# The low part of each weight piece from ScalarE and an accumulating DMA instead of a VectorE subtraction

## The chip, the cores and the metric

The kernel runs on one core of a Trainium2 chip. The metric is the device time of one execution in microseconds (us), lower is better. The engines are named as in the profile: PE (TensorE matmul), PEld (TensorE weight load), DVE (VectorE), ACT (ScalarE), POOL (GpSimd), SP (SyncE).

## What is computed

Two transformer layers over 512 tokens of 1024 channels, float32, batch 1. In short, out of the reference:

```python
x = x + 0.5 * swiglu_ffn(rmsnorm(x, ffn1_norm), ffn1_w_gate, ffn1_w_up, ffn1_w_down)
x = x + hybrid_mixer(rmsnorm(x, mix_norm), w_in, ...)      # sparse attention and gated linear attention
x = x + 0.5 * swiglu_ffn(rmsnorm(x, ffn2_norm), ffn2_w_gate, ffn2_w_up, ffn2_w_down)
x = rmsnorm(x, final_norm)
# second layer: pooling branch and bidirectional mLSTM branch, gated, merged, projected, added to x
swiglu_ffn(x, g, u, d) = (silu(x @ g) * (x @ u)) @ d        # d_ff = 2816
```

Nearly all of the work is the product of activations with weight matrices.

## The kernel before

Channels lie on the partitions and the 512 tokens along the free dimension. TensorE multiplies in float32r, a rounded format. To keep float32 accuracy every operand is cut into a high part (`hi`, the value rounded to float32r) and a low part (`lo`, the rest), and `mm3` makes three matmuls of each product: hi by hi, weight-hi by activation-lo, weight-lo by activation-hi.

All weight matrices are cut on the host into pieces of 128x1024 in the order of use. `load` brings the next piece into a `raw` buffer through SP's DMA queue. `chunk` makes `whi` from it with a copy on ACT (line 107) and `wlo` with a subtraction on DVE (line 108). There are three buffers each of `raw`, `whi` and `wlo`. 253 pieces go through `chunk`; a few others are split elsewhere.

`Tiles.next` hands out the eight 128x128 weight tiles of a piece, one after the other, to `gemm_t`, which makes one 128-channel output of 512 tokens (lines 124 to 126 in `mm3`). So a piece lasts for 24 matmuls of 512 columns. `gemm_nat` takes two pieces at once, and walks over both of them twice, for two token tiles each time: 96 matmuls of 256 columns a pair of pieces. It is called nine times: for `gv` (twice), `gr` (twice), `vn` and `V` (twice two).

The framework's scheduler puts the instructions of each engine in an order of its own. Each engine then runs its instructions strictly in that order, and waits on semaphores for what it needs. The buffers set when a piece can be split: ACT may write the `whi` of a piece when the matmuls of the piece three before it are done, and SP may load into a `raw` buffer when the last reader of it is done.

The products' results go from PSUM through DVE and ACT: in the feed-forward part `ft` (gate times the norm's factor, then Silu), `fv` (up, times that) and `hdh`, `hdl` (the two parts of the product).

Of the kernel before, what the change touches and what calls it, by code (L numbers as in the profile page):

```python
# [10 lines left out]
F32 = mybir.dt.float32  # L11
F32R = mybir.dt.float32r
I32 = mybir.dt.int32
AF = mybir.ActivationFunctionType
ALU = mybir.AluOpType
AX = mybir.AxisListType

P = 128
# [9 lines left out]
MM_BANKS = 4  # L28
UP = 4  # the first up product starts this many tiles behind the gate product
FILL = (0, 2, 4, 6, 8, 10, 13, 16)  # the steps between the heads that carry other products  # L30

# columns of the packed per-channel vectors
VEC = {}
# [10 lines left out]
def kernel(  # L44
# [9 lines left out]
    nc = tc.nc  # L54
# [19 lines left out]

# [1 line left out]
    vs = cp.tile([P, NVEC], F32, name="vs")  # L76
# [16 lines left out]

# [1 line left out]
    state = {"n": 0}  # L95

    def load():
        raw = wp.tile([P, 1024], F32, tag="raw", name="raw", bufs=3)
        nc.sync.dma_start(raw, wst[state["n"]])
        state["n"] += 1  # L100
        return raw

    def chunk(raw=None):
        raw = raw or load()
        hi = wp.tile([P, 1024], F32R, tag="whi", name="whi")
        lo = wp.tile([P, 1024], F32R, tag="wlo", name="wlo")
        act.copy(hi, raw)  # L107
        dve.tensor_sub(lo, raw, hi.bitcast(F32))  # L108
        return hi, lo
# [18 lines left out]
    def gemm_t(tl, ah, al, name="g"):  # L128
        """psum[channel, token] of one 128-wide tile of output channels"""
        o = bank(name, "mm")  # L130
        n = len(ah)
        for k in range(n):
            wh, wl = tl.next()
            mm3(o, wh, wl, ah[k], al[k], k == 0, k == n - 1)
        return o

    def gemm_nat(ah, al, evac):
        """psum[token, channel] of 256 output channels, one token tile after the other"""
        c = [chunk(), chunk()]
        for i0 in range(0, NT, 2):  # L140
            outs = [bank(f"gn{i0 + i}", "mm") for i in range(2)]
            for k in range(KT):
                hi, lo = c[k // 4]
                cs = slice((k % 4) * 256, (k % 4 + 1) * 256)
                for i in range(2):
                    s = slice((i0 + i) * P, (i0 + i + 1) * P)
                    mm3(outs[i][:, :256], ah[k][:, s], al[k][:, s], hi[:, cs], lo[:, cs],
                        k == 0, k == KT - 1)
            for i in range(2):
                evac(i0 + i, outs[i][:, :256])  # L150

    def split(src, g, name, alloc):
        """hi/lo float32r parts of src * g (g a per-partition column or None)"""
        h, l = alloc(name + "h", F32R), alloc(name + "l", F32R)
        split_into(h, l, src, g)
        return h, l
# [8 lines left out]

# [1 line left out]
    def sq_acc(acc, src, first):  # L167
# [13 lines left out]
    def rsqrt_small(src, scale, name, shape=None):  # L181
        """1 / sqrt(src * scale + eps): shifted-exponent seed, three Newton steps"""
        sh = shape or [P, NT]
# [20 lines left out]

# [1 line left out]
    def new_acc():  # L206
# [30 lines left out]
    def normed(gname, acc):  # L237
        """evacuation that splits x * g for the next product and sums the squares"""
        ah, al = [], []

        def evac(d):
            a, b = split(x[d], vcol(gname, d), "x", xs)
            ah.append(a)
            al.append(b)
            sq_acc(acc, x[d], d == 0)
        return ah, al, evac

    # the first gate and up products run along with the loads of x and its split
    raws = []
# [20 lines left out]

    # a column of zeros that is there after the split: the squares come behind it
    zero = cp.tile([P, 1], F32, name="zero")
# [15 lines left out]

# [1 line left out]
    with ExitStack() as mx:  # L290
# [11 lines left out]

        # tables that depend on positions alone
        valid = mt("valid", shape=[P, 1])
# [15 lines left out]

# [1 line left out]
        hid = {}  # L322
# [3 lines left out]
        def compress_blocks(n):  # L326
            pe_n = pe_k if n == "k" else pe_v
            blk = [wtmp("blk", [P, 8, 2, 31]) for _ in range(2)]
            for g in range(2):
# [3 lines left out]
                nc.gpsimd.dma_start(st[64:128, 0:T - 1], src[:, 1:T])  # L333
                # blk[a][:, j, g, n] = st[:, 16 n + 2 (8 a + j)] + pe[:, 8 a + j]
                for a in range(2):
# [34 lines left out]
        with tc.tile_pool(name="gp", bufs=1) as gp:  # L370
# [10 lines left out]

            # 64 channels: both parts of their weights fit one tile, and two passes do
            gat = ga("gat", shape=[64, T])
# [14 lines left out]
            dve.tensor_mul(gat, t, rbc[:64])  # L398
            # decay: cumulative log_sigmoid within 64-token chunks (b) and 128-token pairs (bp)
            zs, es = [], []  # L400
            for c in range(2):
# [6 lines left out]
                zs.append(z), es.append(e)  # L408
            # gates, natural, sigmoid as 1 / (1 + exp(-z))
            o = bank("gt")  # L410
# [17 lines left out]
            for c in range(2):  # L428
# [4 lines left out]
                bp3 = bp.rearrange("p (n s) -> p n s", n=4)  # L433
                # q exp(b), k exp(b_last - b) of even chunks, k exp(bp_last - bp), k exp(-b), q exp(bp)
                qi, kn = ga(f"qin{c}"), ga(f"ktn{c}")
# [23 lines left out]

# [1 line left out]
            S = gt("S", [P, 2, P])  # L461
# [54 lines left out]

# [1 line left out]
            blk = {}  # L518
            for n in ("k", "v"):
                o = gemm_t(tl, ah, al)  # L520
                dve.tensor_mul(kcv[n], o, rbc)
                blk[n] = compress_blocks(n)
            # per head (hi; lo) of the query over 128 rows, (hi; hi) and (lo; lo) of the key
            # (a query carries 1 / slope of its head, so that one distance table serves all)
            def qk_tile(j):
# [39 lines left out]

            # gated, normalised, transposed
            for i in range(NT):
# [11 lines left out]
        with tc.tile_pool(name="np", bufs=1) as np_:  # L579
            # distances in units of 1 / slope: key - query (the query at the last tile), and of the blocks  # L580
            dist = np_.tile([P, T], F32, name="dist")
# [15 lines left out]

            # x += (gated linear attention's half of the output projection), between the heads
            def gla_out(d):
                o = gemm_t(tl, [ogl[0][:, c] for c in range(4)], [ogl[1][:, c] for c in range(4)], "wo")  # L600
                dve.tensor_add(x[d], o, x[d])

            # query tiles by bank: 3; 2 and 0; 1
            GRP = ((3,), (2, 0), (1,))
            OFF = {3: 0, 2: 512, 0: 896, 1: 1024}

            def probs(b, h):
                """exp of the shifted scores of one head, queries on the partitions"""
                j, e = h % 4, h // 4
# [45 lines left out]

# [1 line left out]
            def compressed(i):  # L657
# [40 lines left out]

            # heads 2 c and 2 c + 1 for the output projection
            no = {}  # L700
# [31 lines left out]

# [1 line left out]
            acc = new_acc()  # L734
# [22 lines left out]

# [1 line left out]
    mb = ctx.enter_context(tc.tile_pool(name="mb", bufs=1))  # L759
# [18 lines left out]

    # gates: rows 0-3 forward, 32-35 backward
    R = 36  # L780
# [28 lines left out]
    for src, dst in ((G, Gn), (F, En)):  # L809
        o = bank("gT")  # L810
# [3 lines left out]

    # values of two heads, natural, in two parts, with a column of ones per head
    def values2():
# [12 lines left out]

    # queries and keys: width-5 convolution along the tokens, silu  # L830
    def conv(c):
# [67 lines left out]

    # branch gate sigmoid(o) * silu(z_b)  # L900
    gate = []
# [31 lines left out]

    # merge gates and projections
    def merged(yh, yl, br, into):
# [16 lines left out]

    # pooling branch
    yh, yl = [], []
# [46 lines left out]
    def into_a(c, t, o):  # L1001
# [4 lines left out]
        nl.append(b)  # L1006
        # the residual, tokens on the partitions
        i, g = c // 2, c % 2
# [7 lines left out]

    # output projection, post norm, residual, tokens on the partitions: all weights on chip
    gp2 = []
# [21 lines left out]
    def project(tiles, g):  # L1040
        """o * gain and the sum of o * o of some token tiles, 512 channels"""
        outs = [bank("wo2", "mm") for _ in tiles]
# [32 lines left out]
def _stream(i):  # L1075
    """every weight matrix, cut into [128, 1024] pieces in the order of use"""
    out = []

    def t_tiles(w):
        # [K, M] -> tiles in the order (m, k)  # L1080
        K, M = w.shape
        return w.reshape(K // P, P, M // P, P).transpose(2, 0, 1, 3).reshape(-1, P, P)
# [6 lines left out]
    def nat(w):  # L1089
        # [K, C] -> pieces of 256 columns, four k-tiles each  # L1090
        K, C = w.shape
        a = w.reshape(K // 512, 4, P, C // 256, 256).transpose(3, 0, 2, 1, 4)
        out.append(a.reshape(-1, P, 1024))
# [118 lines left out]
```

## Time and profile before

| what | us |
|---|---|
| median of 3 runs | 1662.3 |
| the runs | 1659.72, 1662.3, 3320.43 |
| span of the profiled execution | 1658.6 |
| PE busy in it | 1636.0 |
| DVE, ACT, POOL busy in it | 888.1, 643.2, 75.8 |

The span goes from the first to the last instruction. The page has no other time for the profiled execution, so its own time is the span and what lies around it; the lowest run is 1.1 us over the span and the median 3.7 us. The run of 3320.43 us is twice the others and is left aside. Instructions that issue DMAs aren't counted as busy. Matmuls overlap in the pipeline: two 512-column matmuls start about 0.23 us apart and are shown with 0.39 us each, so their distance counts and not their length.

### The profile page before, as it was taken

How to read it: one execution, taken by the hardware profiler on the slowest of the kernel's cores; microseconds unless marked ns; L12 is line 12 of the kernel's file. 1: busy time of each engine (PE TensorE's matmuls, PEld its weight loads, DVE VectorE, ACT ScalarE, POOL GpSimd, SP SyncE). 2: the span in 40 equal slices, each digit the busy share in tenths (PEclk: the TensorE clock that was granted, in tenths of full speed). 3: DMA queues.
4: the chain of work that ended last, by engine and by line, in shares of the span. 5: the costliest groups of instructions: out<-in, count | busy, mean ns of one | idle time of the engine just before them, and what ended most of it. 6: DMA issues, size and time to landing. Idle time of an engine off the chain costs nothing.

```text
span 1658.6 us, 20445 instructions
## 1 busy us (share of the span) xinstructions
PE 1636.0 (99%) x8122; PEld 1376.7 (83%) x8122; DVE 888.1 (54%) x1528; ACT 643.2 (39%) x974; POOL 75.8 (5%) x197
## 2 busy tenths in 40 slices
PE   8999999999999999999999999899999999999997
PEld 6888888888789898888888888888988888888886
DVE  6444443336364866544444344688676453466454
ACT  5232232225234554432322333477564332334341
POOL 0000000000100111000000000311000000111000
PEclk9999999999999999999999999999999999999999
DMA  5222222232232100222222232121212222222231
GB/s 181 102 89 102 102 89 102 90 106 80 75 127 77 39 26 26 91 100 99 92 102 97 94 102 91 62 90 51 77 64 77 102 89 89 102 97 95 89 127 51
DMA packets 41663, 146.92 MB, mean 89 GB/s; under 512 B 4704, under 2 KB 5024, under 8 KB 41568
## 3 DMA queue, kind: packets, MB, share of 16 engines
q1 hardware_dynamic: 40608, 143.67, 24.9%
q8 instruction: 64, 1.05, 0.2%
q0 software_dynamic: 384, 1.05, 0.2%
q10 hardware_dynamic: 576, 0.89, 0.2%
q14 instruction: 31, 0.25, 0.0%
HBM read 142.45 MB, written 2.10 MB: 87 GB/s over the span
## 4 chain that ended last, share of the span: by engine, by line
PE 96%; DVE 1%; issue 1%; ACT 1%; POOL 0%; DMA 0%; DVEq 0%; POOLq 0%; ACTq 0%
PE g L126 6%; PE g L125 6%; PE g L124 6%; PE u L125 5%; PE u L124 5%; PE u L126 5%; PE dn L125 5%; PE dn L126 5%; PE dn L124 5%; PE pv L646 2%; PE gn L125 2%; PE gn L126 2%; PE gn L124 2%; PE qk L124 2%; PE mg L124 2%; PE mg L126 2%
## 5 line engine op out<-in xcount | busy, mean ns | idle before, releaser
L107 ACT CAST whi<-raw 128x1024 fp32r<-128x1024 f32 x253 | 266.0, 1052 | 666.5 <-issue 293.6
L108 DVE TENSOR_TENSOR wlo<-raw,whi 128x1024 fp32r<-128x1024 f32 x253 | 313.3, 1239 | 182.0 <-ACT whi L107 178.5
L124 PE MATMUL g<-xh,whi 128*128 128x512 f32 x448 | 176.5, 394 | 6.5 <-ACT xh L163 6.5
L125 PE MATMUL g<-xl,whi 128*128 128x512 f32 x448 | 175.8, 392 | 0.5 <-DVE xl L164 0.5
L126 PE MATMUL g<-xh,wlo 128*128 128x512 f32 x448 | 175.4, 392 | 0.0
L124 PE MATMUL u<-xh,whi 128*128 128x512 f32 x352 | 137.3, 390 | 0.0
L125 PE MATMUL u<-xl,whi 128*128 128x512 f32 x352 | 137.2, 390 | 0.0
L126 PE MATMUL u<-xh,wlo 128*128 128x512 f32 x352 | 137.0, 389 | 0.0
L124 PE MATMUL dn<-hdh,whi 128*128 128x512 f32 x352 | 136.9, 389 | 0.0
L125 PE MATMUL dn<-hdl,whi 128*128 128x512 f32 x352 | 136.9, 389 | 0.0
L126 PE MATMUL dn<-hdh,wlo 128*128 128x512 f32 x352 | 136.9, 389 | 0.0
L124 PEld LDWEIGHTS g<-xh,whi 128*128 128x128 f32 x448 | 84.6, 189 | 24.4 <-ACT xh L163 7.0
L227 DVE TENSOR_TENSOR fv<-u,rbc 128x512 f32<-128x512 f32 x44 | 30.4, 691 | 134.1 <-PE u L126 134.1
L125 PEld LDWEIGHTS g<-xl,whi 128*128 128x128 f32 x448 | 84.5, 189 | 18.5 <-DVE xl L164 1.0
L126 PEld LDWEIGHTS g<-xh,wlo 128*128 128x128 f32 x448 | 84.5, 189 | 17.6
L125 PE MATMUL gn<-wlo,xh 128*128 128x256 f32 x288 | 82.8, 287 | 0.0
L126 PE MATMUL gn<-whi,xl 128*128 128x256 f32 x288 | 82.6, 287 | 0.0
L124 PE MATMUL gn<-whi,xh 128*128 128x256 f32 x288 | 82.6, 287 | 0.0
L224 DVE TENSOR_TENSOR ft<-g,rbc 128x512 f32<-128x512 f32 x44 | 30.4, 691 | 90.8 <-PE g L126 88.9
L125 PEld LDWEIGHTS u<-xl,whi 128*128 128x128 f32 x352 | 66.2, 188 | 13.8
L124 PEld LDWEIGHTS u<-xh,whi 128*128 128x128 f32 x352 | 66.3, 188 | 13.7
L126 PEld LDWEIGHTS u<-xh,wlo 128*128 128x128 f32 x352 | 66.2, 188 | 13.8
(439 smaller groups left out, 3290.2 us busy)
## 6 DMA issues: line engine op xcount, KB each, us to landing
raw<-in_dram SPq DMA_DIRECT2D x266, 512.0 KB, 3.2
x<-in_dram SPq DMA_DIRECT2D x8, 256.0 KB, 5.8
out_dram<-xn SPq DMA_DIRECT2D x8, 256.0 KB, 2.1
post<-in_dram ACTq DMA_DIRECT2D x2, 256.0 KB, 4.0
acc<-kcT POOLq DMA_DIRECT2D x2, 128.0 KB, 3.1
acc<-vcT POOLq DMA_DIRECT2D x2, 128.0 KB, 2.4
acc<-kcT POOLq DMA_DIRECT2D x2, 127.8 KB, 3.9
acc<-vcT POOLq DMA_DIRECT2D x2, 127.8 KB, 3.5
```

What stands on the lines that cost most here:

```text
L107: act.copy(hi, raw)
L108: dve.tensor_sub(lo, raw, hi.bitcast(F32))
L124: pe.matmul(out, lh, rh, start=start, stop=False)
L125: pe.matmul(out, lh, rl, start=False, stop=False)
L126: pe.matmul(out, ll, rh, start=False, stop=stop)
L224: dve.tensor_mul(t, g, rbc)
L227: dve.tensor_mul(v, u, rbc)
L646: pe.matmul(o[:, i * 65:(i + 1) * 65], pt[:, q0:q0 + P], vn[kt][:, b, e, :65], start=(kt == 0), stop=(kt == i))
```

## The change

In `chunk`, the subtraction on DVE is gone. ACT writes `lo` as the copy of `raw` with scale -1, rounded to float32r, which is minus the high part. Then GpSimd issues a DMA that reads `raw` and adds it to `lo`, in place. The rest of the diff takes out comments and shifts lines by two (line 107 becomes 108, line 126 becomes 128); `raw` still has three buffers, the pool's own number.

```diff
     def load():
-        raw = wp.tile([P, 1024], F32, tag="raw", name="raw", bufs=3)
+        raw = wp.tile([P, 1024], F32, tag="raw", name="raw")
         nc.sync.dma_start(raw, wst[state["n"]])
     def chunk(raw=None):
         raw = raw or load()
         hi = wp.tile([P, 1024], F32R, tag="whi", name="whi")
         lo = wp.tile([P, 1024], F32R, tag="wlo", name="wlo")
         act.copy(hi, raw)
-        dve.tensor_sub(lo, raw, hi.bitcast(F32))
+        act.activation(lo, raw, AF.Copy, scale=-1.0)
+        nc.gpsimd.dma_start(lo, raw, accum_op=ALU.add)
         return hi, lo
```

On ACT in the feed-forward part, one round of a gate and an up product (`hdh` belongs to the up product, `ft` to the gate product). Before:

```order
L160 CAST hdh<-fv 128x512
L107 CAST whi<-raw 128x1024
L225 ACTIVATE ft<-ft 128x512
L107 CAST whi<-raw 128x1024
L160 CAST hdh<-fv 128x512
```

and in the changed kernel:

```order
L162 CAST hdh<-fv 128x512
L108 CAST whi<-raw 128x1024
L109 ACTIVATE wlo<-raw 128x1024
L227 ACTIVATE ft<-ft 128x512
L108 CAST whi<-raw 128x1024
L109 ACTIVATE wlo<-raw 128x1024
L162 CAST hdh<-fv 128x512
```

Each `wlo` stands right behind its `whi`, ahead of `ft` and `hdh`.

On ACT in the two calls of `gemm_nat` for `gr`, from the first call's first results on (the numbers are those of buffers). Before:

```order
L558 ACTIVATE gr_3613<-gn_3629,r 128x256
L107 CAST whi<-raw 128x1024
L558 ACTIVATE gr_3614<-gn_3680,r 128x256
L558 ACTIVATE gr_3615<-gn_3681,r 128x256
L107 CAST whi<-raw 128x1024
L558 ACTIVATE gr_3612<-gn_3744,r 128x256
```

and in the changed kernel:

```order
L560 ACTIVATE gr_3695<-gn_3713,r 128x256
L109 ACTIVATE wlo<-raw 128x1024
L108 CAST whi<-raw 128x1024
L560 ACTIVATE gr_3696<-gn_3764,r 128x256
L560 ACTIVATE gr_3697<-gn_3765,r 128x256
L108 CAST whi<-raw 128x1024
L109 ACTIVATE wlo<-raw 128x1024
L560 ACTIVATE gr_3694<-gn_3830,r 128x256
```

The first `wlo` here, that of the second call's second piece, moved ahead of its `whi`.

On PE at the start of the program, where the first gate product `g` and up product `u` run along with the loads of x. Before:

```order
L124 MATMUL g<-xh,whi 128x512
L125 MATMUL g<-xl,whi 128x512
L126 MATMUL g<-xh,wlo 128x512
L124 MATMUL g<-xh,whi 128x512
L125 MATMUL g<-xl,whi 128x512
```

and in the changed kernel:

```order
L126 MATMUL g<-xh,whi 128x512
L127 MATMUL g<-xl,whi 128x512
L126 MATMUL u<-xh,whi 128x512
L127 MATMUL u<-xl,whi 128x512
L128 MATMUL g<-xh,wlo 128x512
L126 MATMUL g<-xh,whi 128x512
```

The first matmul that reads `wlo` moved from the third place to the fifth; later `g` and `u` alternate as they did.

At the mLSTM gates (lines 789 to 801 before) the cast of a next piece stood on ACT between two of the three steps that make `lf`; in the changed kernel the cast and the new copy stand behind the third. The order on PE is otherwise nearly the same.

On POOL, the first 68 accumulating DMAs stand in one row, and the later ones stand between POOL's other work.

## Rows read from the trace of the kernel before

**Rows 1.** The page: busy us, share of the span, number of instructions.

```profile
PE 1636.0 (99%) x8122; PEld 1376.7 (83%) x8122; DVE 888.1 (54%) x1528; ACT 643.2 (39%) x974; POOL 75.8 (5%) x197
```

**Rows 2.** Busy us by stage (engine order as in Rows 1), then clock, DMA share, GB/s.

```profile
20.00:376.00 356.00, 356.00 (x1584) 294.59 (x1583) 156.28 (x192) 107.22 (x131) 1.73 (x12) 1.00 0.28 99
```

**Rows 3.** Groups of instructions: busy us, mean ns, idle before and its releasers.

```profile
L108 DVE TENSOR_TENSOR wlo<-raw,whi 128x1024 fp32r<-128x1024 f32 x253 | 313.3, 1239 | 182.0 <-ACT whi L107 178.5 <-PE bc L199 1.7 <-issue 0.3
L107 ACT CAST whi<-raw 128x1024 fp32r<-128x1024 f32 x253 | 266.0, 1052 | 666.5 <-issue 293.6 <-PE g L125 144.8 <-PE dn L125 114.6
```

**Rows 4.** Timeline, feed-forward: start us, us, engine; ACT rows, then PE where a piece changes.

```profile
153.54 1.06 ACT L107 CAST whi<-raw 128x1024 fp32r<-128x1024 f32 x1 [3.86 <-issue]
158.98 1.06 ACT L107 CAST whi<-raw 128x1024 fp32r<-128x1024 f32 x1 [3.11 <-PE g L125]
164.42 1.06 ACT L107 CAST whi<-raw 128x1024 fp32r<-128x1024 f32 x1 [3.86 <-issue]
...
164.18 0.39 PE L126 MATMUL u<-xh,wlo 128*128 128x512 f32 x1
164.40 0.39 PE L124 MATMUL g<-xh,whi 128*128 128x512 f32 x1
```

**Rows 5.** DMA queues (packets, MB, share of 16 engines) and issues (KB, median us).

```profile
q1 hardware_dynamic: 40608, 143.67, 24.9%
q0 software_dynamic: 384, 1.05, 0.2%
...
raw<-in_dram SPq DMA_DIRECT2D x266, 512.0 KB, 3.2
```

**Rows 6.** The eight POOL-issued DMAs of 128 KB into `acc`, from issue to landing.

```profile
DMA to landing us min/median/max: 2.2/3.2/4.4
```

**Rows 7.** Timeline, start of the program; the last row is the 48th matmul.

```profile
4.74 1.04 ACT L107 CAST whi<-raw 128x1024 fp32r<-128x1024 f32 x1 [2.20 <-DMA raw<-in_dram]
6.47 0.79 PE L124 MATMUL g<-xh,whi 128*128 128x512 f32 x1 [6.47 <-ACT xh L163]
8.35 0.63 PE L126 MATMUL g<-xh,wlo 128*128 128x512 f32 x1
8.77 0.63 PE L124 MATMUL g<-xh,whi 128*128 128x512 f32 x1
12.79 0.47 PE L126 MATMUL u<-xh,wlo 128*128 128x512 f32 x1
20.86 0.39 PE L126 MATMUL u<-xh,wlo 128*128 128x512 f32 x1
```

**Rows 8.** Timeline: casts of second pieces for `gv`, `gr`, `V`; first matmuls on their `wlo`.

```profile
410.51 1.04 ACT L107 CAST whi<-raw 128x1024 fp32r<-128x1024 f32 x1
415.74 0.28 PE L125 MATMUL gn<-wlo,xh 128*128 128x256 f32 x1
511.89 1.05 ACT L107 CAST whi<-raw 128x1024 fp32r<-128x1024 f32 x1 [2.44 <-issue]
517.53 0.28 PE L125 MATMUL gn<-wlo,xh 128*128 128x256 f32 x1
1176.19 1.05 ACT L107 CAST whi<-raw 128x1024 fp32r<-128x1024 f32 x1 [1.34 <-PE gn L126]
1181.87 0.28 PE L125 MATMUL gn<-wlo,xh 128*128 128x256 f32 x1
```

**Rows 9.** The chain that ended last (start us, us, what), around the mLSTM gates.

```profile
1041.37 1.23 DVE wlo L108
1051.68 0.95 ACT whi L107
```

**Rows 10.** PE behind its wait there: idle and releaser in brackets; 256-column distances.

```profile
1062.17 0.64 PE L812 MATMUL gT<-ident,gi 36*128 36x36 f32 x4 [5.15 <-DVE gi L801]
1066.95 0.41 PE L126 MATMUL gn<-whi,xl 128*128 128x256 f32 x1
1067.17 0.41 PE L124 MATMUL gn<-whi,xh 128*128 128x256 f32 x1
1067.76 0.28 PE L124 MATMUL gn<-whi,xh 128*128 128x256 f32 x1
1067.87 0.28 PE L125 MATMUL gn<-wlo,xh 128*128 128x256 f32 x1
```

## The prediction

> **What bounds the kernel now.** The busy shares come first: PE is busy for 1636.0 of 1658.6 us, DVE for 54%, ACT for 39% [rows 1]. The kernel is a row of matmuls, and what other engines do costs only where PE waits: 22.6 us in all, most of them at the start and at the gates of the mLSTM [rows 7, 10]. The table by stage says it more sharply: in the first feed-forward part PE has not 0.1 us of idle time in 356 us, and the DMA engines are busy 28% of that time [rows 2].
>
> Then the rhythm of a piece. The casts of `whi` start at 153.54, 158.98 and 164.42 us, so a piece lasts 5.44 us (24 matmuls, 0.227 us apart). The cast at 164.42 starts as PE leaves the up product's piece at 164.40 [rows 4]: ACT waits for the buffer and for nothing else, and fills it for the piece that PE will begin two pieces later. A piece therefore has 2 x 5.44 = 10.88 us from the cast to its first matmul, 11.3 us to the first matmul that reads `wlo` (the third). The old way takes 1.05 us for the cast and 1.24 us for the subtraction [rows 3], and the rest is slack.
>
> **The change part by part.**
>
> **Removed:** 253 subtractions of 1239 ns, 313 us of DVE. DVE isn't what PE waits for in the dense stages, so this gives nothing there. At the mLSTM gates a chain of small steps on DVE and ACT ends in a PE wait of 5.15 us [rows 10]. A `wlo` of 1.23 us lies in it on DVE and a `whi` of 0.95 us on ACT [rows 9]; in the new order the first is gone from DVE and both copies stand behind the chain's ACT steps. I count the two, 2.2 us, as a gain of 2 us.
>
> **Added on ACT:** 253 copies at the cast's 1.05 us, 266 us, so ACT rises to some 909 us, 55%. In the feed-forward round it has 4 x 1.05 + 2 x 0.62 us of work in 10.88 us, and the order puts `whi`, `wlo` first when a buffer comes free. `ft` and `hdh` come 1 us later; their readers, a piece later, don't notice. I count nothing; what covers it is the piece of slack.
>
> **Added as DMA:** the question is two prices. Call X the time from the end of ACT's `wlo` to the sum's landing, and E the time that the sum takes of all 16 DMA engines.
>
> E: q1 moved 143.67 MB in 24.9% of 1658.6 us, so 512 KB (0.524 MB) cost 1.5 us of all engines. Q0, SBUF to SBUF and issued by POOL, moved 1.05 MB in a rounded 0.2%, between 1.2 and 2.1 us for 512 KB [rows 5]. No row shows an accumulation. Its floor is one such pass, 1.5 us; its ceiling is a full pass each for reading `raw`, reading `wlo` and writing, 4.6 us. A plain copy already reads and writes each byte within its one pass, and the sum adds one read, so I take two passes, 3.0 us. With the load that is 4.5 of 5.44 us: the DMA engines go from 28% to about 83% in the dense stages, and still keep up. The point from which they don't is E = 3.9 us. The Trainium skill (Collectives: The Full Stack, "The bandwidth ceiling: the fold count and why AG ≠ RS ≠ AR") says that the add in a DMA costs nothing of itself, but the second source halves the rate, 62.28 against 32.35 GB/s; no run here shows it yet, and by it E would be 1.93 x 1.5 = 2.9 us and the sum the same.
>
> X: POOL's DMAs of 128 KB land 2.2 to 4.4 us after the issue, median 3.2 [rows 6]. Of this some 0.4 us is data (a quarter of a pass), which leaves 2.8 us that don't grow. The floor of X is one plain transfer, 3.2 us, which is also what a 512 KB load takes [rows 5]. The ceiling is 2.8 + 4.6 + 1.5 for a weight load that runs on the same engines at the same time, 8.9 us, and 0.5 for the issue of twice as many rows, 9.4 us. I take 2.8 + 3.0 + 1.2 of sharing = 7.0 us, nearest to the median of rows 6 with two passes.
>
> What X meets, place by place:
> - Dense stages: 11.3 - 2 x 1.05 = 9.2 us of room. X = 7.0 is hidden. `raw` is now held until the sum lands: cast start + 2.1 + 7.0, then a load of 3.2 us, 12.3 us after the cast, while ACT wants it 3 x 5.44 = 16.3 us after. Hidden, too; SP's queue has nothing else in it.
> - Start: `whi` runs from 4.74 us, `wlo` to 6.85, the sum lands at 13.85 where the old `wlo` was read at 8.35. PE has four matmuls to do before that and then 44 for the two products. The clock is low there: matmuls are 0.42 us apart from 8.35 us and 0.23 us apart after 12.79 us, 6.3 us after the first one [rows 7]. If the low stretch comes again, 15 matmuls at 0.43 us and 29 at 0.227 end at 26.9 us against 21.1: 5.8 us lost (2.7 us at the full clock).
> - Second pieces in `gemm_nat`: a pair of pieces lasts only 96 x 0.12 = 11.5 us, and the buffer for the next pair's second piece comes free at three quarters of it. `gv`: `wlo` could end at 411.56 and is read at 415.74, 4.2 us of room; `gr` 512.94 to 517.53, 4.6 us; the second `V` pair 1177.24 to 1181.87, 4.6 us [rows 8]. At X = 7.0 PE waits 2.8 + 2.4 + 2.4 = 7.6 us; `vn` comes out about even, and the first `V` pair waits for the gates anyway. After the 5.15 us wait at the gates, matmuls of 256 columns are 0.21 us apart until 1067.2 us and 0.11 to 0.12 after [rows 10]: 5 us at half speed, 2.5 us lost. The waits here are half as long; I take 0.5 us each, 1.5 us (0 to 7.5).
> - POOL is nearly idle, 75.8 us [rows 1], and issues one DMA in 5.44 us. Its queue is in order, and some sums stand behind masks and additions that wait for DVE or ACT; the products that need those pieces come later still in PE's order, so I count nothing.
>
> Sum: -2 + 5.8 + 7.6 + 1.5 = +12.9 us, a span of 1671.5 us. The median of the runs lies 3.7 us over the span of before: **1675 us**. A measurement of this kernel can tell about 2%, 33 us, from no change. Between X = 5.5 and 9.2 us the same sum runs from about 1668 to 1690 us.
>
> **The rivals.**
>
> *A cheap sum.* X under 5.5 us: only the start loses, 2 to 4 us, `gemm_nat` at most 3, and the gates give back 2: 1662 to 1668 us. For it: the floor of 3.2 us. Against it: this floor has one pass and no neighbour. The Trainium skill (DMA: Bandwidth & Descriptors, "Anatomy of one DMA — SWDGE (gpsimd) path") fits a POOL-issued DMA as 2.0 us and its bytes at 436 GB/s. By that rule, with two passes, X = 2.0 + 2 x 1.2 = 4.4 us and the time 1664 us; the trace only half agrees, since for 128 KB it gives 2.3 us and the row has a median of 3.2.
>
> *The DMA engines become the bound* (slower). It decides from E = 3.9 us, 2.6 passes. Then every dense piece lasts 1.5 + E in place of 5.44 us. Of the 253 pieces, 18 go to `gemm_nat` and a few lie between the attention heads; some 230 are dense. At three passes it is 6.1 us a piece, 0.65 x 230 = 150 us, and with the start and `gemm_nat` about 1830 us. For it: no row prices the addition, and the busy share leaves only 0.9 us of 5.44. Against it: the read and the write of a copy overlap.
>
> *The latency becomes the bound* (slower). Above X = 9.2 us the loop of three buffers (5.44 + 2.1 + X - 0.45 us) is longer than three pieces, and each further us costs 0.33 us a piece, 77 us in all, beside the 28 us that X = 9.2 costs at the start and in `gemm_nat`: X = 9.4 gives some 1705 us, X = 10.5 some 1795. For it: my ceiling touches it, and with 83% busy engines transfers queue. Against it: 2 us of room at X = 7.
>
> *Faster by over 2%* would need 33 us, more than the 22.6 us that PE has idle, so only a change that no row hints at could bring it.
>
> *The change doesn't take the work off*: the order shows no subtraction of `wlo` left on DVE, but POOL's in-order queue may hold a sum back behind a mask that waits for DVE, as the old order held it behind DVE's own work. A few such waits at X each would give 1685 to 1700 us; I keep this within the forecast's range.
>
> **How the numbers follow.** Forecast (X 5.5 to 9.2, E under 3.9) 0.45, a cheap sum 0.17, the engines 0.19, the latency 0.16, faster by over 2% 0.03. So: within 2% 0.62, slower 0.35, faster 0.03. The range goes from the floor of the cheap sum, 1661, to three passes, 1830, which leaves out the dearer ends of the two slow rivals and the gain, under 2 in 10. The likeliest case alone is 1668 to 1690.
>
> **What would show it.** Right: PE busy without a gap in 20 to 376 us, the sum 6 to 9 us after `wlo` ends, the DMA share there near 0.8, PE waiting for the DMA of `wlo` at the start and three times 2 to 3 us in `gemm_nat`, ACT near 909 us. Wrong: a DMA share near 1 in the dense stages or a `wlo` that is waited for at every piece (the slow rivals); no waits on `wlo` in `gemm_nat` (the cheap sum); POOL holding sums back behind a mask, which I gave nothing.

## The result: 1680.5 us, 1.1% over before

The changed kernel took 1680.49 us (median; 1679.17 to 1684.77), beside 1661.95 us for the kernel before on the same chip (a median that counts its run of 3320.43 us, which the ratio leaves aside): a ratio of 1.0114, 95% interval 1.0098 to 1.0131. That is 18.5 us more, a small loss that the interval keeps clear of zero, and within the 2% that counts as no change here. Its profiled execution has a span of 1678.6 us, 20.0 us over before's 1658.6.

The page of the changed kernel answers to [rows 1, 3, 5], with the same columns: engines, two groups, queues, issues.

```profile
PE 1644.1 (98%) x8122; PEld 1380.2 (82%) x8122; DVE 594.9 (35%) x1275; ACT 873.6 (52%) x1225; POOL 289.9 (17%) x450
...
q0 software_dynamic: 36816, 133.71, 45.0%
q1 hardware_dynamic: 40608, 143.67, 25.9%
...
L110 POOL DMA_DIRECT2D wlo<-raw x253 | 218.6, 865 | 1136.4 <-ACT wlo L109 1091.0
L109 ACT ACTIVATE wlo<-raw 128x1024 fp32r<-128x1024 f32 x253 | 266.2, 1052 | 18.2 <-PE gn L127 14.8
...
raw<-in_dram SPq DMA_DIRECT2D x266, 512.0 KB, 4.4
wlo<-raw POOLq DMA_DIRECT2D x253, 512.0 KB, 5.8
```

DVE lost its 293 us, ACT gained 230 (266.2 in the copies' group, but a copy starts some 0.1 us before the cast ahead of it ends), and POOL shows 218.6 us for issuing. The sums took 45.0% of 1678.6 us on all 16 DMA engines for 133.71 MB, so 0.524 MB cost 2.96 us. A weight load now lands after 4.4 us where it took 3.2 [rows 5].

The same stretch as in [rows 2], in the table by stage, says what this costs in the feed-forward part: nothing.

```profile
20.00:376.00 356.00, 355.80 (x1575) 294.21 (x1574) 81.24 (x127) 166.17 (x195) 55.08 (x64) 1.00 0.84 193
```

PE misses 0.2 us of 356, with the DMA engines busy for 84% of the time instead of 28%. The loss must lie elsewhere. Cutting both traces at the same places of the program finds it: the start up to `la`'s first matmul, to the first `cmp`, to the first `ogT`, and then the second feed-forward part up to the `gates`. First the kernel before (busy us of PE, PEld, DVE, ACT, POOL; then clock, DMA share, GB/s):

```profile
0.00:382.70 382.70, 375.74 (x1657) 309.56 (x1658) 173.01 (x228) 122.72 (x152) 2.22 (x17) 1.00 0.31 107
382.70:468.00 85.30, 84.86 (x485) 69.30 (x485) 43.26 (x86) 35.51 (x82) 8.16 (x13) 1.00 0.21 69
468.00:526.00 58.00, 58.00 (x383) 53.27 (x382) 31.76 (x41) 25.86 (x45) 1.05 (x3) 1.00 0.34 119
526.00:1033.00 507.00, 505.80 (x2587) 428.46 (x2587) 261.28 (x489) 190.18 (x286) 20.46 (x33) 1.00 0.23 80
```

and the changed kernel, cut at the same matmuls:

```profile
0.00:389.70 389.70, 375.81 (x1653) 308.77 (x1653) 93.46 (x158) 185.68 (x220) 61.77 (x86) 1.00 0.85 197
389.70:480.40 90.70, 89.19 (x489) 72.28 (x489) 35.18 (x79) 42.97 (x90) 16.21 (x22) 0.96 0.50 120
480.40:544.10 63.70, 60.62 (x384) 54.67 (x383) 18.30 (x29) 36.90 (x56) 9.45 (x13) 0.97 0.74 177
544.10:1050.20 506.10, 505.43 (x2586) 429.08 (x2585) 175.03 (x413) 259.70 (x361) 85.94 (x109) 1.00 0.69 158
```

The stages cost +7.0, +5.4, +5.7 and -0.9 us. From the gates to the first `gT` it is -2.2 (29.2 to 27.0 us), from there to the first `zb` +4.2 (164.6 to 168.8), and the rest +0.8: together 20.0. At the start all 7 us are idle time of PE. In the two mixer stages 4.2 us are idle, and for 7.0 us PE is busy longer, at a mean granted clock of 0.96 and 0.97 where before has 1.00.

PE's waits in the changed kernel (engine, line, released by; us, times, longest):

```profile
PE g L126 <- ACT xh L165: 8.1, 1, 8.1
PE g L128 <- DMA wlo<-raw: 6.7, 2, 4.7
PE gT L814 <- DVE gi L803: 5.7, 1, 5.7
PE gn L127 <- DMA wlo<-raw: 2.6, 4, 1.1
```

The first is the wait for the first data, 6.47 us before [rows 7]. Of PE's waits for a sum, one lies at the start (4.7 us), four in `gemm_nat` (2.6 us in all), and one in a place that the prediction did not price (1.9 us). The timeline of the start, with POOL's and PE's rows, answers to [rows 7]:

```profile
6.34 1.05 ACT L109 ACTIVATE wlo<-raw 128x1024 fp32r<-128x1024 f32 x1
...
7.71 1.01 POOL L110 DMA_DIRECT2D wlo<-raw  x1 [6.24 <-ACT wlo L109]
...
8.06 0.80 PE L126 MATMUL g<-xh,whi 128*128 128x512 f32 x1 [8.06 <-ACT xh L165]
16.49 0.80 PE L128 MATMUL g<-xh,wlo 128*128 128x512 f32 x1 [4.75 <-DMA wlo<-raw]
28.15 0.39 PE L128 MATMUL u<-xh,wlo 128*128 128x512 f32 x1
```

The copy ends at 7.39 us and its sum is read at 16.49, 9.1 us later, while the loads of x are in flight. The 48th matmul starts at 28.15 instead of 20.86 us: 7.3 us late.

The place not priced is the compression of keys and values, between 480 and 503 us. The timeline there, ACT, then POOL, then PE:

```profile
488.17 1.05 ACT L108 CAST whi<-raw 128x1024 fp32r<-128x1024 f32 x1 [1.08 <-DMA raw<-in_dram]
489.12 1.05 ACT L109 ACTIVATE wlo<-raw 128x1024 fp32r<-128x1024 f32 x1
...
490.47 0.92 POOL L110 DMA_DIRECT2D wlo<-raw  x1 [12.25 <-ACT wlo L109]
...
489.40 3.68 PE L348 MATMUL cmp<-blk,raw 128*128 128x62 f32 x32
496.82 0.50 PE L128 MATMUL g<-xh,wlo 128*128 128x512 f32 x1 [1.91 <-DMA wlo<-raw]
```

The `cmp` products read their weights straight from `raw` buffers and hold them. So the next pieces cannot be loaded ahead: load, cast, copy and sum run one behind the other, ACT waits for the load, and PE for the sum.

The clock shows on PE's own rows, just behind the narrow `la` and `gt` matmuls. PE has no wait ahead of them:

```profile
389.75 1.98 PE L405 MATMUL la<-gat,cws 16*128 16x512 f32 x4
391.66 0.46 PE L414 MATMUL gt<-ident,gat 64*128 64x64 f32 x4
...
393.20 0.63 PE L126 MATMUL g<-xh,whi 128*128 128x512 f32 x1
393.63 0.63 PE L127 MATMUL g<-xl,whi 128*128 128x512 f32 x1
...
396.26 0.39 PE L128 MATMUL g<-xh,wlo 128*128 128x512 f32 x1
396.49 0.39 PE L126 MATMUL g<-xh,whi 128*128 128x512 f32 x1
```

Matmuls of 512 columns stand 0.43 us apart, and 0.23 us apart from 396.26: the lower of the two levels, 1.2 GHz, and then 2.4 GHz again. There are three such stretches in the mixer, from 392, 468 and 498 us, each some 3.4 us long by the granted clock, so each loses 1.7 us. The third begins 1.4 us behind PE's wait of 1.91 us for a sum; the other two have no such wait near them. The profile of the kernel before has none of the three; its only low stretch in mid-span is behind the gates [rows 10].

But a profile is one execution, and the clock differs between executions of one kernel. In 50 more executions of the kernel before, run beside the experiments, the mean granted clock lies between 0.992 and 0.997, and the time goes with it, from 1667.62 us at the low end to 1659.75 us at the high end. Before's profile has 0.997, so it shows one of the best of these executions; the four of the changed kernel have 0.990 to 0.995. By the mean of all executions, 0.9954 against 0.9928, the clock makes some 4 of the 18.5 us (an estimate: the difference times 1660 us).

### The profile page after: what moved, and what is told of

Read it like the earlier page. It is cut to its first block, busy times and chain, and to the rows that moved or that the text cites. A ratio compares the mean times of both kernels' runs of the same rounds, so it can differ in the third digit from the quotient of the medians.

```text
span 1678.6 us, 21098 instructions
## 1 busy us (share of the span) xinstructions
PE 1644.1 (98%) x8122; PEld 1380.2 (82%) x8122; DVE 594.9 (35%) x1275; ACT 873.6 (52%) x1225; POOL 289.9 (17%) x450
## 3 DMA queue, kind: packets, MB, share of 16 engines
q0 software_dynamic: 36816, 133.71, 45.0%
q8 instruction: 64, 1.05, 0.2%
## 4 chain that ended last, share of the span: by engine, by line
PE 91%; DMA 4%; issue 2%; ACT 1%; DVE 1%; POOL 0%; DVEq 0%; POOLq 0%; ACTq 0%; SPq 0%
PE g L128 5%; PE g L126 5%; PE g L127 5%; PE u L128 5%; PE u L126 5%; PE u L127 5%; PE dn L128 5%; PE dn L127 5%; PE dn L126 5%; DMA wlo<-raw 3%; PE pv L648 2%; PE wo L128 2%; PE wo L126 2%; PE qk L126 2%; PE mg L128 2%
## 5 line engine op out<-in xcount | busy, mean ns | idle before, releaser
L110 POOL DMA_DIRECT2D wlo<-raw x253 | 218.6, 865 | 1136.4 <-ACT wlo L109 1091.0
L109 ACT ACTIVATE wlo<-raw 128x1024 fp32r<-128x1024 f32 x253 | 266.2, 1052 | 18.2 <-PE gn L127 14.8
L128 PEld LDWEIGHTS dn<-hdh,wlo 128*128 128x128 f32 x352 | 66.1, 188 | 14.1 <-DMA wlo<-raw 0.5
```

The source lines that it names most:

```text
L109: act.activation(lo, raw, AF.Copy, scale=-1.0)
L110: nc.gpsimd.dma_start(lo, raw, accum_op=ALU.add)
L128: pe.matmul(out, ll, rh, start=False, stop=stop)
```

## The experiments

The theory at this point: the loss is the sum's latency at three kinds of place (the start, `gemm_nat`, the compression), with the clock on top; the dense stages pay nothing. The first rival: the sums slow everything a little, through the shared DMA engines. The second: the loss is not the sum's but comes with what the scheduler and ACT's second copy did. All kernels are edits of the changed one.

**1. The subtraction back for the first four pieces** (`start_sub`).

```diff
+        state["c"] += 1
+        if state["c"] - 1 in SUB:              # SUB = set(range(4))
+            dve.tensor_sub(lo, raw, hi.bitcast(F32))
+        else:
             act.activation(lo, raw, AF.Copy, scale=-1.0)
             nc.gpsimd.dma_start(lo, raw, accum_op=ALU.add)
```

> The first four pieces are split by the old DVE subtraction, the other 249 by the accumulating DMA. In the changed kernel the 48th matmul of the first two products starts at 28.15 us against 20.86 before. If the start is a loss by itself (my theory), the time falls by 6 to 7 us from 1680.5, to 1673 to 1675, and the profile has that matmul near 21 us. Rival: the start's loss is taken over by the next wait (pieces 4 and 5, loaded late because the engines are busy with sums), and the time stays over 1678.

Measured: 1674.04 us, ratio 1.0069 (1.0054 to 1.0084), 6.4 us below the changed kernel. In the profile the 48th matmul is back at 20.89 us and the first `la` at 381.7, 8.0 us earlier, but the span is only 4.7 us shorter. So 3.4 us are lost again further on, where two waits on sums (1.1 us at 397, 2.6 us at 530) and low-clock stretches (430 to 433, 450 to 454 and 488 to 495 us) came at other places.

**2. The subtraction back for pieces 66 to 95** (`mixer_sub`): as above, with `SUB = set(range(66, 96))`, the pieces from the end of the first feed-forward part through the mixer's projections.

> The 30 pieces of the hybrid mixer (numbers 66 to 95) are split by the old subtraction, the rest by the DMA. Theory: the landmarks say that the span lost 11 us between the first gate product of the mixer and the end of its projections, through waits of PE for sums (some 4 us) and three stretches of low clock of 3.5 us each. So the time falls by 9 to 11 us, to 1670 to 1672, and the low stretches at 392, 468 and 498 us go. Rival: the low clock there has nothing to do with the sums; then the stretches stay and the gain is only 4 to 5 us, 1675 to 1677.

Measured: 1671.69 us, ratio 1.0065 (1.0047 to 1.0083), 8.8 us below the changed kernel, though its start is 1.2 us slower (`la` at 391.0). The table by stage, from the first `la` to the first `cmp` and on to the first `ogT`:

```profile
391.00:476.30 85.30, 84.83 (x485) 69.26 (x485) 43.20 (x86) 35.51 (x82) 8.18 (x13) 1.00 0.22 68
476.30:534.40 58.10, 58.10 (x384) 53.37 (x383) 31.81 (x41) 25.93 (x45) 1.06 (x3) 1.00 0.35 118
```

These are before's 85.30 and 58.00 us again, at a clock of 1.00, and PE's order is before's there. So the 11 us of these two stages come from the new way of making `wlo` in them and from nothing upstream. But the edit gives back three things at once: no sums, no second copy on ACT, and the old order of the matmuls.

**3. The sum left out** (`no_sum`): ACT's copy stays and the accumulating DMA is gone, so the low part stays minus the high part.

```diff
         act.activation(lo, raw, AF.Copy, scale=-1.0)
-        nc.gpsimd.dma_start(lo, raw, accum_op=ALU.add)
```

> Leaves the accumulating DMA out: the low part is only the negative high part. ACT has all its 253 copies, DVE none of the subtractions. Theory: ACT's added 266 us are hidden but for 1 to 2 us at the start (the first xh comes behind the copy), so 1660 to 1664, no difference from before that can be told. Rival: the copies on ACT cost in the mixer and the mLSTM, where ACT is read from directly; then 1666 to 1672.

Measured: 1668.26 us, ratio 1.0031 (1.0023 to 1.0040). The forecast of 1660 to 1664 missed: 6 us of the 18 stay without a single sum. They lie in the mixer ahead of the compression (`la` at 383.6 us, 0.9 late; the first `cmp` at 473.2, 5.3 late), with low-clock stretches at 387 to 390 and 431 to 435 us. From there to the first `ogT` the kernel takes 58.1 us, as before does, where the changed kernel takes 63.7. So the 5.6 us lost in that stage, its low-clock stretch among them, come only with the sums (PE's order in it differs, too), and 4.4 of the 5.4 us of the stage ahead of it come without any.

**4. The DMA as a plain copy** (`plain_copy`): the same DMA without the addition, so the low part is the raw weight.

```diff
-        nc.gpsimd.dma_start(lo, raw, accum_op=ALU.add)
+        nc.gpsimd.dma_start(lo, raw)
```

> The DMA copies raw over the low part and doesn't add (so the low part is raw itself). Theory: the sum's data time of 2.96 us of all engines is two passes, so a plain copy has 1.5 us; the share of queue q0 falls from 45.0% to 22 to 24%, the DMA share of the dense stages from 0.85 to 0.57, the landing from 5.8 to 4.0 to 4.5 us, and the time to 1670 to 1675. Rival: the second read was cheap and the addition or POOL's descriptors make the time; then the share falls by less than a third and the landing stays over 5 us.

Measured: 1673.32 us, ratio 1.0068 (1.0054 to 1.0081). Its page, the two queues and the issue:

```profile
q1 hardware_dynamic: 40608, 143.67, 26.5%
q0 software_dynamic: 36816, 133.71, 22.4%
...
wlo<-raw POOLq DMA_DIRECT2D x253, 512.0 KB, 2.9
```

The plain DMA takes 22.4% of the engines for the same bytes where the accumulating one takes 45.0%: the addition costs one more pass. Its landing has a median of 2.9 us, beside 5.8, and is shorter than the 4.0 to 4.5 us expected. The 7 us between this kernel and the changed one go with that second pass; how they divide between its latency and its load on the engines is not shown. The start still loses nearly as much (48th matmul at 27.41 us): there the first plain DMA, too, takes 8.2 us from issue to landing, so the long landing at the start is not the addition's.

**5. The subtraction back at the start, in the mixer and for eight pieces of `V`** (`both_sub`): `SUB` holds 0 to 3, 66 to 95, 163 to 166 and 179 to 182; 211 pieces keep their sums.

> Old subtraction for the first four pieces, the mixer's 30 and the two groups of four V pieces (numbers 163 to 166 and 179 to 182); the accumulating DMA for the other 211, nearly all of them in dense stages. Theory: the sums cost nothing in dense stages, so all that is left is 0 to 2 us: 1660 to 1664, the same as before. PE's order in the mixer is that of before, and there is no low clock there. Rival: DMA traffic or ACT's load cost a little everywhere; then 1666 or more.

Measured: 1663.55 us, ratio 1.0008 (0.9998 to 1.0017). Its table by stage, dense stretch:

```profile
20.00:376.00 356.00, 355.95 (x1583) 294.30 (x1582) 84.60 (x133) 163.56 (x192) 55.31 (x74) 1.00 0.84 190
```

So 211 sums at a DMA share of 0.84 cost at most 3 us by the interval, and none that can be told from zero. The first rival falls: the whole loss sits in some 42 pieces and in the order of matmuls that comes with them. One part of the expectation failed: PE's order in the mixer is before's, and the clock was still low there once, from 438 to 441 us. No edit here is faster than the kernel before.

**6. No low part at all** (`alias`): no copy, no DMA, no subtraction for the pieces of `chunk`; the matmuls that read `wlo` read `whi`.

```diff
-        act.activation(lo, raw, AF.Copy, scale=-1.0)
-        nc.gpsimd.dma_start(lo, raw, accum_op=ALU.add)
-        return hi, lo
+        return hi, hi
```

> The low part is left out altogether: the matmuls read the high part in its place; no subtraction, no copy, no DMA. The order on PE in the mixer is that of the changed kernel (13 wide matmuls between the sums of squares and the broadcast in place of 17, 7 after the first scores of linear attention in place of 12). Theory by the order: PE's clock falls to half where narrow matmuls stand closer together, with no sum at all; so two or three low stretches of 3.5 us between 380 and 510 us, and a time of 1661 to 1666, over before, though three kinds of work are gone. Rival by the waits: the clock falls because PE waits for sums or copies; then no low stretch there, and 1655 to 1659.

Measured: 1663.34 us, ratio 1.0004 (0.9994 to 1.0015). With all of the work in question gone the kernel is no faster than before, so no way of making `wlo` could have gained more than a few us. The order of PE is the changed kernel's at `la`, but the clock there is 1.00; it is low only at 428 to 431 us, once where two or three times were expected. The 12 executions of this one kernel have mean clocks from 0.991 to 0.997 and times from 1666.58 to 1659.36 us.

**7. Both writes, no DMA** (`both_write`): DVE's subtraction and then ACT's copy over it, so the low part ends as minus the high part. ACT has its second copy, DVE keeps its load.

```diff
         act.copy(hi, raw)
+        dve.tensor_sub(lo, raw, hi.bitcast(F32))
         act.activation(lo, raw, AF.Copy, scale=-1.0)
-        nc.gpsimd.dma_start(lo, raw, accum_op=ALU.add)
```

> DVE subtracts as before, then ACT writes the negative copy over it; no DMA (the low part is only the negative high part). The order on PE is that of before at the sums of squares and the decay products (17 wide matmuls), and that of the changed kernel in linear attention (7). Theory by the order: full clock at 380 to 395 us, and a low stretch between 425 and 475 us. Rival, that ACT's copies bring the low clock: both places are low. Time 1662 to 1670 by either.

Measured: 1666.62 us, ratio 1.0025 (1.0014 to 1.0035), with no low clock behind `la` but three low stretches later in the mixer (428 to 431, 448 to 452, 458 to 462 us). The kernels differ in how many wide matmuls (of 256 or 512 columns) stand between narrow ones. In the profiles so far, the low clock behind `la` came in three of the five kernels whose order has 13 wide matmuls between the norm's statistics and the broadcast, as the changed kernel's has, and in none of the four with 17, as before's has. In the linear attention, an order with 7 wide matmuls between its narrow groups had a low stretch in all six kernels, one with 12 in one of three; but `dve_first`, run later (experiment 12), has 7 and no low stretch there.

One profile a kernel is thin evidence, and the mean clock over all executions adds to it: 0.995 to 0.996 in the three kernels with 17 and 12, 0.993 to 0.9945 in the six with 7. So the clock tends to be lower with an order in which narrow matmuls stand closer, and it needs no sum. What exactly lets it fall stays open: the same order fell in some kernels and held in others, and executions of one kernel differ.

**8. Half a pass more on POOL's queue** (`extra_256k`): behind each sum, POOL stores half of `raw` to DRAM, which nobody reads.

```diff
         nc.gpsimd.dma_start(lo, raw, accum_op=ALU.add)
+        state["c"] += 1
+        nc.gpsimd.dma_start(scr[state["c"]], raw[:, :512])
```

> The changed kernel, and behind each sum POOL issues one more DMA that stores half of raw, 256 KB, into an unused DRAM tensor: half a pass, 0.75 us of all engines. The dense stages have 0.85 x 5.44 = 4.62 us of DMA work a piece, so 5.37 of 5.44 us with it. Theory (engines as a bound from 5.44 us a piece): just hidden in the dense stages, where PE waits less than 5 us in all 356; the time is 1681 to 1695. Rival (latency): with engines at 99% transfers queue, the sum takes over 9.2 us from the copy, and PE waits at every piece: over 1710.

Measured: 1775.05 us, ratio 1.0678 (1.0664 to 1.0692): far outside the theory's range and within the rival's, over 1710 us. The table by stage and POOL's wait:

```profile
20.00:376.00 356.00, 343.66 (x1493) 277.48 (x1492) 79.19 (x124) 157.98 (x187) 88.59 (x122) 1.00 0.90 227
...
POOL scr_dram L114 <- DMA raw<-in_dram: 968.6, 209, 10.5
```

The share is 0.90 and not 1. POOL, whose queue is in order, waits at the store for a load, 209 times, and the sums stand behind it. From the copy's end to the landing a sum now takes 8.0 us at the median and over 9.2 us in 87 of 253, as the rival says, but not because transfers queue on full engines: from issue to landing it is 5.5 us, less than in the changed kernel. So the price is, as far as these rows show, that of a held queue, and the engines' edge is not measured by this.

**9 and 10. Half a pass and a full pass more on SP's queue** (`d2d_256k`, `d2d_512k`), meant to load the engines without holding a tile or POOL: a copy between DRAM and DRAM behind each weight load.

```diff
         nc.sync.dma_start(raw, wst[state["n"]])
+        nc.sync.dma_start(scr[state["n"]], wst[state["n"]][:64])     # [:128] in d2d_512k
```

> After, with a further DMA behind each weight load on SP's queue: a copy from DRAM to DRAM of 64 rows of 4 KB of the same piece, which nobody reads and which touches no tile. It adds half a pass, 0.75 us of all 16 engines for each piece, without holding a buffer or POOL's queue. The sum and the load take 4.6 of 5.44 us in the dense stages after; here they would take 5.4. Theory (the engines are an edge that has not been reached: nothing is lost until their work fills the piece): right at the edge, 1681 to 1705 us, share over 0.95. Rival (transfers queue long before the engines are full, so after itself already pays for its 85%): each piece loses some 0.2 to 0.7 us, 1730 to 1830 us.

> As the kernel with 256 KB, with 128 rows: 1.5 us of all 16 engines more for each piece than in after, 6.1 us of work for a piece of 5.44. Theory (the engines bound a dense piece as soon as their work is longer than its matmuls): each of some 230 dense pieces takes 0.66 us longer, about 1830 us, 1800 to 1860, with a share near 1 and PE waiting for weights at every piece. Rival (copies between DRAM and DRAM don't share the engines with the sums as plain passes do): under 1760 us.

Measured: 2202.12 us, ratio 1.3236 (1.3168 to 1.3304), and 3698.32 us, ratio 2.2256 (2.2223 to 2.2290). Both theory and rival miss by far, and the kernel with 512 KB shows why. Its timeline, one gate piece:

```profile
226.24 0.33 SPq L100 DMA_DIRECT2D raw<-in_dram  x1
...
233.30 0.39 PE L130 MATMUL g<-xh,wlo 128*128 128x512 f32 x1
233.73 0.69 DVE L228 TENSOR_TENSOR ft<-g,rbc 128x512 f32<-128x512 f32 x1 [13.52 <-PE g L130]
234.45 0.63 ACT L229 ACTIVATE ft<-ft 128x512 f32<-128x512 f32 x1 [13.06 <-DVE ft L228]
234.99 1.03 ACT L110 CAST whi<-raw 128x1024 fp32r<-128x1024 f32 x1
235.92 1.05 ACT L111 ACTIVATE wlo<-raw 128x1024 fp32r<-128x1024 f32 x1
```

ACT's cast of the next piece stands behind `ft` of the gate product in ACT's order, while in the changed kernel's order it stands ahead of it. So the cast waits until PE is done with the piece, and cast, copy, sum and matmuls no longer overlap: 15.9 us a piece (sums issued at 205.81 and 221.68). The DMA share falls to 0.35 from 30 to 386 us, with sums that land after a median of 4.5 us. One added DMA had moved the scheduler's order; nothing was learnt of the engines' edge, and it stays open.

**11. The copy for the low part first** (`lo_first`): ACT writes `lo` ahead of `hi`.

```diff
-        act.copy(hi, raw)
         act.activation(lo, raw, AF.Copy, scale=-1.0)
+        act.copy(hi, raw)
         nc.gpsimd.dma_start(lo, raw, accum_op=ALU.add)
```

> After, with ScalarE writing the negative high part first and the high part behind it, so that the sum starts 1.05 us earlier against the matmuls that need it. Theory (the start and the second pieces lose what the sum's latency exceeds their room): the start gains about 1 us, each wait on a sum in the attention part and gemm_nat up to 1 us: 1674 to 1678 us. Rival (what is lost in the attention part is the order of the matmuls and the clock, not the latency): 1679 to 1682 us, or wherever a new order takes it.

Measured: 1681.16 us, ratio 1.0117 (1.0102 to 1.0133): the rival's range, no gain. The 48th matmul is at 28.16 us, as late as before the edit, though each sum may start 1.05 us earlier; PE's waits on sums are 15.8 us in all instead of 9.3. The order moved with the edit, so what an earlier copy is worth by itself is not shown; here it gained nothing.

**12. The copy on DVE** (`dve_first`): DVE writes the negative high part, ACT only casts; the sums stay.

```diff
+        dve.tensor_scalar_mul(lo, raw, -1.0)
         act.copy(hi, raw)
-        act.activation(lo, raw, AF.Copy, scale=-1.0)
         nc.gpsimd.dma_start(lo, raw, accum_op=ALU.add)
```

> After, with VectorE writing the negative high part in place of ScalarE, ahead of ScalarE's cast; the sums stay. Theory (neither ScalarE's 1.05 us for each piece nor VectorE's counts in the dense stages; only the sum's latency and the order of the matmuls do): 1672 to 1681 us, POOL's DMA-issuing instruction at 0.8 to 0.9 us as in after. Rival (the Trainium skill, SBUF - State Buffer, on VectorE's fast modes holding GpSimd off the shared port while it writes descriptors): the issuing instruction gets longer by VectorE's time on the copy, up to 2 us, the sum lands later, and the start and the attention part lose some 1 us at each wait: 1684 to 1690 us.

Measured: 1678.98 us, ratio 1.0105 (1.0090 to 1.0120), the same as the changed kernel within its runs. ACT is back at 639 us and DVE at 748. The tile `wlo` in this kernel (ns min/median/max):

```profile
L108 DVE TENSOR_SCALAR wlo<-raw x253: 673/685/1579, 5.0 to 1608.3; 128x1024 fp32r<-128x1024 f32 x127
L110 POOL DMA_DIRECT2D wlo<-raw x253: 851/860/1162, 6.0 to 1609.5; - x127
```

POOL's issue keeps its 860 ns. The Trainium skill (SBUF — State Buffer, "Who interferes with whom") says that a VectorE operation in a two-port mode holds GpSimd off the port on which it writes a DMA's descriptors; no lengthening shows here, but each copy ends before its own issue begins, so this run hardly puts the rule to the test. What it does show is that the time does not depend on which engine makes the copy: ACT's added 266 us is hidden, as the prediction had it.

## Why the prediction was right, and which terms were off

The forecast was 1675 us by way of "dense stages hidden, the start and a few waits lost", and the measured 1680.5 lies within its own range of 1668 to 1690. Step by step:

**The DMA's price E** was taken as two passes, 3.0 us, and measured 2.96; experiment 4 shows the second pass alone (45.0 against 22.4%). The engines went to 84% where 83% was forecast. The rule of the Trainium skill (Collectives: The Full Stack, "The bandwidth ceiling: the fold count and why AG ≠ RS ≠ AR") that a second source halves the rate agrees with this trace, 2.0 where it gives 1.93. The rival by three passes falls.

**The latency X** was taken as 7.0 us. Over all 253 pieces its median is 6.2 (mostly 0.3 us from the copy to the issue, then a median of 5.8 to the landing), and at the start it is 9.1. POOL's queue, which I gave nothing, holds back few sums: ten are issued over 1 us behind their copy, the worst 4.9 us at the gates, and PE waits for none of these. The Trainium skill's fit (DMA: Bandwidth & Descriptors, "Anatomy of one DMA — SWDGE (gpsimd) path") made X an estimated 4.4 us and speaks for the cheap sum; the trace does not agree with two passes (5.8 from issue alone), and for the plain DMA it is near (3.2 by the fit, 2.9 measured).

**Dense stages, nothing lost:** shown by the 355.80 of 356 us, and by experiment 5. ACT's copies hidden there: experiment 12.

**The start, +5.8 forecast, +7.0 to 7.3 measured.** The mechanism is the one forecast, and experiment 1 gives 6.4 of it back. Two things are larger: the copy stands ahead of the split of x in ACT's order and the load landed later, so the first matmul starts at 8.06 and not at 6.47 us; and the sum lands among the loads of x, at 16.4 and not at 13.85 us. One is smaller: behind it 9 matmuls run at the lower clock (16.49 to 20.43 us), where I had 15.

**`gemm_nat`, +7.6 forecast, +2.6 measured: the mis-sized term.** I subtracted before's room from X, piece by piece, as if the order around it stayed. At the four waits the room from the copy's end to PE's need is 6.6, 4.9, 6.6 and 4.9 us where I had 4.2 to 4.6, and X is 6.8, 5.5, 7.2 and 6.0 us. The wait near 426 us answers to a sum that was issued at 421.29, since the next one was issued at 425.60 and no sum lands in less than 4.5 us; ACT had made that low part ahead of its high part:

```profile
419.94 1.06 ACT L109 ACTIVATE wlo<-raw 128x1024 fp32r<-128x1024 f32 x1
420.90 1.03 ACT L108 CAST whi<-raw 128x1024 fp32r<-128x1024 f32 x1
```

So the scheduler gave back some of the latency, here by putting the copy ahead of the cast; X itself was clearly shorter at two of the four.

**The clock, +1.5 forecast, about +5 in the profile** (some +4 by the mean of all executions), in the mixer and not only behind waits: three stretches of 1.7 us. I had tied the low clock to waits, from [rows 10]. Experiments 3, 6 and 7, which have no sums and keep low stretches, show that it falls without them; only the third stretch, behind a wait for a sum, fits the tie.

**The compression, nothing forecast, +2.4 measured:** PE idles 3.1 us between `cmp` and `ogT`, of which 0.7 is one of the `gemm_nat` waits. I had looked for rooms only where a piece is split in time, and not where `raw` buffers are held by somebody else.

**The gates, -2 forecast:** the chain from the gates to `gT` is 2.2 us shorter, as worked out from [rows 9], and yet nothing is gained:

```profile
1077.18 0.64 PE L814 MATMUL gT<-ident,gi 36*128 36x36 f32 x4 [5.71 <-DVE gi L803]
1077.75 0.58 PE L127 MATMUL gn<-wlo,xh 128*128 128x256 f32 x1
```

PE waits 5.71 us where it waited 5.15 [rows 10], because the scheduler put `gT` ahead of 18 matmuls of the next pair that used to fill this time. They come behind it, and the following stage is 4.2 us longer.

The sum was +12.9 and the span came out at +20.0. Terms that were too high (`gemm_nat`) and too low (clock, compression, gates) partly cancel, so that the time lies this near to the forecast is in part luck. Luck is also in the 3.7 us from the span to the median: an execution takes 1.6 to 2.0 us over its own span, and the rest was that before's profile fell on a high clock.

What experiments share out is coarser: 6.4 us to the start and 8.8 to the mixer's pieces; with both back and `V` too the loss is gone (1.5 us, interval touching zero). Of the mixer's share some 4 to 5 us need no sum (experiment 3): they lie ahead of the compression, and an order of the matmuls and a lower clock come with them. Why the clock falls at one place in one kernel and not in another is not settled.

## What to carry to other kernels

Where PE has no gap, relieving another engine buys nothing: leaving all of this work out (experiment 6) gave the time of before. What a longer path costs is found by its room at each place: plenty in a steady stage of three buffers, none at the start of the program, behind products that hold the shared buffers, and in stages whose pieces are short. And any edit to what feeds PE lets a scheduler reorder PE itself; compare the orders first, and read a stage's result only from kernels whose order there is known. Differences of a few us are read from many executions, not from one profile each.

## What the runs showed of the hardware

An accumulating DMA of 512 KB from SBUF into SBUF, float32, takes 2.96 us of 16 engines, twice the plain one's (45.0 against 22.4% of the span); it lands 5.8 us after its issue, the plain one 2.9. POOL's issuing instruction takes 0.86 us for the first and 0.53 us for the second. DMA engines at 84% in a steady stage do not slow it, though the weight loads beside them take 4.4 us instead of 3.2. The granted clock can fall to 1.2 GHz for some 3.4 us while PE is busy the whole time, behind narrow matmuls such as `la` and `gt`, and how often it does differs between executions of one kernel (mean clock 0.992 to 0.997 over 50 executions of the kernel before, 1667.62 to 1659.75 us).
